# Splits of the transposes moved ahead of the work around them, and eight loads begun from ScalarE's queue, in a two-layer hybrid encoder

## The chip, the cores and the metric

The kernel runs on one core of one Trainium2 chip. The metric is the time of one execution on the device, in microseconds (us), as the median of several runs; lower is better. One further run was taken with the hardware profiler, and all rows shown come from it.

A core has engines that each work through their own instructions strictly in the order in which these were laid down: TensorE (PE in the profile, its weight loads PEld), VectorE (DVE), ScalarE (ACT), GpSimd (POOL) and SyncE (SP). Between engines only semaphores order the work. An engine whose next instruction waits does nothing, even if a later one could run.

## The reference, cut to what matters

A sequence of 512 tokens with 1024 features goes through two layers. Each layer is a token mixer and a channel mixer (FFN), each with a normalisation ahead of it and one behind it:

```python
for layer in range(DEPTH):                       # 2
    hn = rms_norm(x, norm_mix_pre[layer])
    m = retention_na_mixer(hn, ...) if layer % 2 == 0 else ssd_mixer(hn, ...)
    x = x + rms_norm(m, norm_mix_post[layer])
    f = conv_geglu_ffn(rms_norm(x, norm_ffn_pre[layer]), ...)
    x = x + rms_norm(f, norm_ffn_post[layer])
```

The second mixer is the state space layer: its result y (512 x 2048) is multiplied by an output matrix, and what comes out is m. The FFN is an up-projection to 2 x 2816 columns, a convolution over three tokens, gelu(gate) * value, and a down-projection.

## The kernel before, in words

The 512 tokens are four tiles of 128 (t = 0 to 3), which lie on the partitions in `E.x`. A product needs its left operand with features on the partitions, so each normalised tile is transposed on TensorE. All products are made from two-part numbers: `split` (lines 79 to 82) takes a float32 tile and makes a rounded part `hi` with a ScalarE copy (L81) and a rest `lo` with a VectorE subtraction (L82), which needs `hi` first. A product is then three matmuls (`mm3`, L86 to L88): high by high, high by low, low by high. In the rows, `whi` and `wlo` are the parts of a weight, `xh` and `xl` those of the transposed tile, `hh` and `hl` parts that lie in the FFN's own buffers, and `wst` is the buffer in which a weight lands.

From one stage to the next a tile goes through this chain, all of it per tile t and some of it per half of 512 features:

- `post_half` (L144): the sum of squares of a half of m on ScalarE (L119, `junk`, with the result `ssm`), and m times the gain on VectorE (L150, `mg`).
- `post_norm` (L167): 1/rms from both sums (`v_m`, L109, on VectorE, then `r_m`, L111, on GpSimd), and `x = mg * r_m + x` for both halves (L175, VectorE).
- `norm` (L121): sum of squares of x (L119, ScalarE, `ssx`), 1/rms (`v_x`, L109; `r_x`, L111), and `xs = x * r_x * gain` for both halves (L131, VectorE).
- `turn` (L134): for each half four transposes on TensorE into a PSUM tile `pt` (L140), and the split of `pt` into `xh` (L81, ScalarE) and `xl` (L82, VectorE).

`finish` (L152) runs these for the tiles by small tables of steps: x is `post_norm`, s is `norm`, t is `turn`. At the end of the state space layer the table is `TAIL`; the turns of tiles 2 and 3 come from a list `late`, which the next FFN flushes between its first products. Those first products are cut by columns: the FFN first takes tokens 0 to 255 (tiles 0 and 1) of four products: with its first pair of weights (`mm_9234`, `mm_9235` in the built program), then with its second pair (`mm_9236`, `mm_9237`, whose weight parts are `hh` and `hl` and lie where the state space layer's `mg` tiles lay), then tokens 256 to 511 of all four. TensorE's order holds tile 2's transposes between the first and the second pair, and tile 3's among the second pair's products.

In the state space layer's last stage (`out_tile`, L815), `E.x` serves as the accumulator of the output product, and x itself waits in device memory (`xd`). For each tile and half, VectorE adds the last group's product to the accumulator and puts m elsewhere (L828), and then a load brings x back into `E.x` (L829). `post_norm` of the tile needs both loads. All loads of the kernel, these eight and the weights', are begun from SyncE's queue, in order.

The order on each engine is made by a scheduler when the program is built. It follows the order in which the code is written; what is written under `high_priority(n)` ranks n places further ahead. The splits of weights have stood under `high_priority(60)`; the splits in `turn` under none.

Of the kernel before, what the change touches and what calls it, by code (L numbers as in the profile page):

```python
# [25 lines left out]
class Env:  # L26
# [107 lines left out]
    def turn(self, t):  # L134

        nc = self.nc
        for h, xs in enumerate(self.xs[t]):
            pt = self.px.tile([P, 4, P], F32, name="pt", tag="px")
            for j in range(4):
                nc.tensor.transpose(pt[:, j], xs[:, j * P:(j + 1) * P], self.ident)  # L140
            o = (slice(None), slice(h * 4, h * 4 + 4), slice(t * P, (t + 1) * P))
            self.split(self.xh[o], self.xl[o], pt)

    def post_half(self, st, t, n, ps, g_post, eng=None, m=None):  # L144

# [407 lines left out]
def mixer1(E, w_dt, w_fm, cw, dtc, cols, mask, w_out, g_post_row, done):  # L553
# [4 lines left out]
    nc, tc = E.nc, E.tc  # L558
    C = P
    H, H2 = SSD_H, 2 * SSD_H  # L560
    with ExitStack() as ctx:
# [14 lines left out]
        xd = E.dram.tile([NT, P, D], F32, name="xd")  # L576
# [231 lines left out]
        def out_mm(o, t, ws):  # L808
            ps = E.mm.tile([P, 512], F32, name="mm")
            tt = slice(t * P, (t + 1) * P)  # L810
            for k in range(4):
                yh, yl = o["y"][k]
                E.mm3(ps, yh[:, tt], yl[:, tt], *ws[k], k == 0, k == 3)
            return ps

        def out_tile(o, n, t, ws, fin=None, ps=None):
            g = o["g"]
            ns = slice(n * 512, n * 512 + 512)
            if ps is None:
                ps = out_mm(o, t, ws)  # L820
            acc, r = E.x[:, t, ns], o["r"][:, t:t + 1]
            if g == 0:
                nc.scalar.activation(acc, ps, AF.Identity, scale=r)
            elif g < NG - 1:
                nc.vector.scalar_tensor_tensor(acc, ps, r, acc, op0=ALU.mult, op1=ALU.add)
            else:
                m = three.tile([P, 512], F32, name="m", tag="e")
                nc.vector.scalar_tensor_tensor(m, ps, r, acc, op0=ALU.mult, op1=ALU.add)  # L828
                nc.sync.dma_start(acc, xd[t, :, ns])  # L829
                fin(t, n, m)  # L830

        def out(o, n):
            ws = E.wunit(w_out[o["g"], n, 0]) + E.wunit(w_out[o["g"], n, 1])
            for t in range(NT):
                out_tile(o, n, t, ws)
# [48 lines left out]
        def fin(t, n, m):  # L884
            E.post_half(st, t, n, m, g_post, None, four.tile([P, 512], F32, name="mg", tag="z"))
# [7 lines left out]
        for t in range(NT):  # L893
            for n in range(2):
                out_tile(gs[-1], n, t, ws[n], fin, first[n] if t == 0 else None)
            E.finish(TAIL[t], st, done)
# [146 lines left out]
```

## Time and profile before

| what | value |
|---|---|
| median of 3 runs | 1437.23 us |
| lowest and highest of them | 1435.54 and 1437.54 us |
| time of the profiled execution | 1435.78 us |
| its span, from the first to the last instruction | 1434.0 us |
| TensorE busy | 1398.5 us, 98% of the span |
| VectorE busy | 946.3 us, 66% |
| ScalarE busy | 720.3 us, 50% |
| GpSimd busy | 60.6 us, 4% |

How to read the rows: a row of the timeline has the start in us from the beginning of the span, the duration, the engine, the line, the operation, what it writes and reads, and a count where equal instructions were merged. In brackets stands the idle time of the engine just before, and what ended it. In the row of a window stand its length, then for each engine its busy time and number of instructions, then the clock that was granted to TensorE as a share of full speed (PEclk), then the transfers. Matmuls overlap in their pipeline, so their pace is read from the distance of their starts, not from their durations.

### The profile page before, as it was taken

To read this page: it belongs to the slowest core of one execution; us is meant where nothing else is said; L and a number is where in the kernel's file an instruction comes from. 1 tells how busy PE (TensorE), PEld (TensorE's weight loads), DVE (VectorE), ACT (ScalarE), POOL (GpSimd) and SP (SyncE) were. 2 spreads that over 40 slices of the span, in tenths; PEclk is the share of its full clock that TensorE was granted. 3 is DMA by queue.
4 is the path that set the end of the run, shared out by engine and by line. 5 is a ranking of instruction groups with operands and counts; after the bars stand their busy time and mean duration, and the time that the engine had idled before them with its cause. 6 is when DMAs were issued, how large, how long until landed. Compare 5 with 4: busy or idle time off the path is not lost.

```text
span 1434.0 us, 18009 instructions
## 1 busy us (share of the span) xinstructions
PE 1398.5 (98%) x6832; PEld 1141.0 (80%) x6832; DVE 946.3 (66%) x1486; ACT 720.3 (50%) x1192; POOL 60.6 (4%) x67
## 2 busy tenths in 40 slices
PE   7999999999999999999999999999889999999998
PEld 6877777898888888888777787777678888888886
DVE  7368888666566552357889786999886666564242
ACT  5356665454444431334888766577544444443230
POOL 0010110100000000000000000000110000000000
PEclk9999999999999999999999999999999999999999
DMA  7443232233233333332556354345432233333241
GB/s 255 146 141 92 85 96 77 83 108 102 89 98 95 102 94 97 120 107 95 159 180 184 111 176 131 95 153 162 143 120 87 90 100 94 100 89 102 89 132 59
DMA packets 56950, 166.34 MB, mean 116 GB/s; under 512 B 7200, under 2 KB 7968, under 8 KB 56864
## 3 DMA queue, kind: packets, MB, share of 16 engines
q1 hardware_dynamic: 56864, 165.20, 37.2%
q8 instruction: 54, 0.88, 0.2%
q14 instruction: 32, 0.26, 0.1%
HBM read 157.57 MB, written 5.51 MB: 114 GB/s over the span
## 4 chain that ended last, share of the span: by engine, by line
PE 80%; DVE 9%; ACT 5%; DMA 3%; issue 2%; POOL 0%; SPq 0%; DVEq 0%; POOLq 0%; ACTq 0%
PE mm L86 24%; PE mm L87 24%; PE mm L88 24%; DMA pb<-pd 1%; DVE wlo L82 1%; PE st L719 1%; DVE xf L683 1%; PE pt L140 1%; PE y L449 1%; PE pi L762 1%; DMA wst<-in_c_out 1%; PE pt L663 1%; PE py L782 1%; DVE ti L766 1%; DVE yl L795 0%
## 5 line engine op out<-in xcount | busy, mean ns | idle before, releaser
L88 PE MATMUL mm<-xl,whi 128*128 128x512 f32 (+2 forms) x1216 | 463.9, 382 | 4.0 <-DVE xl L82 3.8
L86 PE MATMUL mm<-xh,whi 128*128 128x512 f32 (+2 forms) x1216 | 464.0, 382 | 1.5 <-ACT z L689 0.7
L87 PE MATMUL mm<-xh,wlo 128*128 128x512 f32 (+2 forms) x1216 | 463.4, 381 | 1.4 <-DVE wlo L82 1.4
L82 DVE TENSOR_TENSOR wlo<-wst,whi 128x1024 fp32r<-128x1024 f32 (+1 forms) x208 | 255.5, 1229 | 198.0 <-ACT whi L81 195.8
L81 ACT CAST whi<-wst 128x1024 fp32r<-128x1024 f32 (+1 forms) x208 | 217.3, 1045 | 191.4 <-PE mm L87 119.6
L88 PEld LDWEIGHTS mm<-xl,whi 128*128 128x128 f32 (+1 forms) x1216 | 228.6, 188 | 48.4 <-DVE xl L82 4.5
L86 PEld LDWEIGHTS mm<-xh,whi 128*128 128x128 f32 (+1 forms) x1216 | 229.0, 188 | 46.8 <-issue 2.4
L87 PEld LDWEIGHTS mm<-xh,wlo 128*128 128x128 f32 (+1 forms) x1216 | 229.0, 188 | 45.2 <-DVE wlo L82 2.7
L227 DVE SCALAR_TENSOR_TENSOR cv<-mm,cwt,cv 128x511 f32<-128x511 f32 x88 | 65.7, 747 | 95.2 <-ACT cv L226 94.9
L86 PE MATMUL mm<-whi,hh 128*128 128x512 f32 x288 | 112.0, 389 | 0.0
L87 PE MATMUL mm<-whi,hl 128*128 128x512 f32 x288 | 112.0, 389 | 0.0
L88 PE MATMUL mm<-wlo,hh 128*128 128x512 f32 x288 | 112.0, 389 | 0.0
L226 ACT ACTIVATE cv<-mm,cwt 128x512 f32<-128x512 f32 x88 | 68.4, 777 | 39.8 <-PE mm L88 39.8
L81 ACT CAST hh<-cv 128x512 fp32r<-128x512 f32 x44 | 27.3, 621 | 100.5 <-DVE cv L235 100.3
L233 ACT ACTIVATE cv<-cv 128x512 f32<-128x512 f32 x44 | 27.8, 633 | 85.2 <-DVE cv L228 85.2
L228 DVE SCALAR_TENSOR_TENSOR cv<-mm,cwt,cv 128x511 f32<-128x511 f32 x88 | 66.0, 750 | 3.0
L744 ACT ACTIVATE ds<-um,tok,ddt 128x128 f32<-128x128 f32 x128 | 55.7, 484 | 16.1 <-DVE e L747 15.7
L88 PEld LDWEIGHTS mm<-wlo,hh 128*128 128x128 f32 x288 | 54.1, 188 | 11.3
L87 PEld LDWEIGHTS mm<-whi,hl 128*128 128x128 f32 x288 | 54.1, 188 | 11.2
L86 PEld LDWEIGHTS mm<-whi,hh 128*128 128x128 f32 x288 | 54.1, 188 | 11.2
L82 DVE TENSOR_TENSOR hl<-cv,hh 128x512 fp32r<-128x512 f32 x44 | 30.5, 693 | 28.9 <-ACT hh L81 28.9
L741 ACT ACTIVATE e<-pb,tok 128x128 f32<-128x128 f32 x128 | 43.0, 392 | 11.7 <-DMA pb<-pd 10.2
(236 smaller groups left out, 1945.6 us busy)
## 6 DMA issues: line engine op xcount, KB each, us to landing
wst<-in_f_up SPq DMA_DIRECT2D x88, 512.0 KB
wst<-in_f_down SPq DMA_DIRECT2D x44, 512.0 KB
wst<-in_c_fm SPq DMA_DIRECT2D x40, 512.0 KB
pb<-pd SPq DMA_DIRECT2D x64, 256.0 KB
wst<-in_ab_fm SPq DMA_DIRECT2D x20, 512.0 KB
gain<-yd SPq DMA_DIRECT2D x32, 256.0 KB
wst<-in_c_out SPq DMA_DIRECT2D x16, 512.0 KB
gain<-in_norms SPq DMA_DIRECT2D x8, 512.0 KB
```

The costliest lines, as they stand in the source:

```text
L81: self.nc.scalar.copy(hi, src)
L82: self.nc.vector.tensor_tensor(lo, src, hi.bitcast(F32), op=ALU.subtract)
L86: mm(out, lh, rh, start=first, stop=False)
L87: mm(out, ll, rh, start=False, stop=False)
L88: mm(out, lh, rl, start=False, stop=last)
L140: nc.tensor.transpose(pt[:, j], xs[:, j * P:(j + 1) * P], self.ident)
L226: nc.scalar.activation(o, ps, AF.Identity, scale=w(1), bias=w(3))
L227: nc.vector.scalar_tensor_tensor(o[:, 1:], ps[:, :S - 1], w(0), o[:, 1:], op0=ALU.mult, op1=ALU.add)
L228: nc.vector.scalar_tensor_tensor(o[:, :S - 1], ps[:, 1:], w(2), o[:, :S - 1], op0=ALU.mult, op1=ALU.add)
L233: nc.scalar.activation(g, g, AF.Gelu_apprx_tanh)
L741: nc.scalar.activation(e[:, c], pb[0][:, cc], AF.Identity, scale=-1.0, bias=tok[:, 0, c, h:h + 1])
L744: nc.scalar.activation(ds[:, c], um, AF.Identity, scale=ddt[:, c, h:h + 1], bias=tok[:, 1, c, H + h:H + h + 1])
```

## The change

Two edits. In `turn`, the split of a transposed tile is put under `high_priority(100)`, so that it ranks ahead of the splits of weights (60) and of what stands up to a hundred places before it. In `out_tile`, the eight loads that bring x back are begun from ScalarE's queue and no longer from SyncE's.

```diff
             o = (slice(None), slice(h * 4, h * 4 + 4), slice(t * P, (t + 1) * P))
-            self.split(self.xh[o], self.xl[o], pt)
+            with self.tc.high_priority(100):
+                self.split(self.xh[o], self.xl[o], pt)
...
                 nc.vector.scalar_tensor_tensor(m, ps, r, acc, op0=ALU.mult, op1=ALU.add)
-                nc.sync.dma_start(acc, xd[t, :, ns])
+                nc.scalar.dma_start(acc, xd[t, :, ns])
                 fin(t, n, m)
```

No instruction is added or removed; the numbers of lines behind the first edit rise by one. Orders change in three kinds of places: at the start of the program, in VectorE's part of the two changes of stage inside it (from the first mixer to its FFN, from that FFN to the state space layer, where TensorE's and ScalarE's orders stay as they were), and at the state space layer's end, where all engines but GpSimd are touched. SyncE also begins a few loads in another order at the start and where the state space layer begins.

The first place is VectorE at the start of the program. `wlo_107` and `wlo_114` are the rests of the first two weights, `pt_135` and `pt_142` the two halves of tile 0's transposes, `pt_160` and `pt_167` those of tile 1. Before:

```order
L82 TENSOR_TENSOR wlo_107<-wst_104,whi_106 128x1024
L82 TENSOR_TENSOR xl_99<-pt_135,xh_98 128x4x128
L82 TENSOR_TENSOR xl_99<-pt_142,xh_98 128x4x128
L82 TENSOR_TENSOR wlo_114<-wst_111,whi_113 128x1024
L82 TENSOR_TENSOR xl_99<-pt_160,xh_98 128x4x128
L82 TENSOR_TENSOR xl_99<-pt_167,xh_98 128x4x128
```

And now:

```order
L82 TENSOR_TENSOR xl_99<-pt_135,xh_98 128x4x128
L82 TENSOR_TENSOR xl_99<-pt_142,xh_98 128x4x128
L82 TENSOR_TENSOR wlo_107<-wst_104,whi_106 128x1024
L82 TENSOR_TENSOR xl_99<-pt_160,xh_98 128x4x128
L82 TENSOR_TENSOR xl_99<-pt_167,xh_98 128x4x128
L82 TENSOR_TENSOR wlo_114<-wst_111,whi_113 128x1024
```

Each weight's rest now stands behind the two rests of a tile.

The second place is VectorE at the end of the state space layer, from the split of tile 0's second half (`pt_9107`) to that of tile 1's first half (`pt_9173`). `m_9127` and `m_9148` belong to tile 3, `mg_9057` and `mg_9078` to tile 2, `xs_9037` and `xs_9039` to tile 1; `wlo_9211` is the rest of the FFN's second weight, `v_m_9083` is of tile 2, `v_x_9033` of tile 1 and `v_x_9092` of tile 2. Before:

```order
L82 TENSOR_TENSOR xl_99<-pt_9107,xh_98 128x4x128
L131 SCALAR_TENSOR_TENSOR xs_9037<-x_97,r_x_9035,gain_8969 128x512
L131 SCALAR_TENSOR_TENSOR xs_9039<-x_97,r_x_9035,gain_8969 128x512
L82 TENSOR_TENSOR wlo_9211<-wst_9208,whi_9210 128x1024
L109 TENSOR_SCALAR v_m_9083<-ssm0_9058,ssm1_9079 128x1
L828 SCALAR_TENSOR_TENSOR m_9127<-mm_9114,rg_8945,x_97 128x512
L175 SCALAR_TENSOR_TENSOR x_97<-mg_9057,r_m_9085,x_97 128x512
L175 SCALAR_TENSOR_TENSOR x_97<-mg_9078,r_m_9085,x_97 128x512
L150 TENSOR_TENSOR mg_9130<-m_9127,gain_8881 128x512
L828 SCALAR_TENSOR_TENSOR m_9148<-mm_9135,rg_8945,x_97 128x512
L109 TENSOR_SCALAR v_x_9092<-ssx_9089 128x1
L82 TENSOR_TENSOR xl_99<-pt_9173,xh_98 128x4x128
```

And now:

```order
L82 TENSOR_TENSOR xl_99<-pt_9107,xh_98 128x4x128
L176 SCALAR_TENSOR_TENSOR x_97<-mg_8998,r_m_9026,x_97 128x512
L176 SCALAR_TENSOR_TENSOR x_97<-mg_9019,r_m_9026,x_97 128x512
L82 TENSOR_TENSOR wlo_9211<-wst_9208,whi_9210 128x1024
L829 SCALAR_TENSOR_TENSOR m_9127<-mm_9114,rg_8945,x_97 128x512
L109 TENSOR_SCALAR v_x_9033<-ssx_9030 128x1
L829 SCALAR_TENSOR_TENSOR m_9148<-mm_9135,rg_8945,x_97 128x512
L131 SCALAR_TENSOR_TENSOR xs_9037<-x_97,r_x_9035,gain_8969 128x512
L131 SCALAR_TENSOR_TENSOR xs_9039<-x_97,r_x_9035,gain_8969 128x512
L151 TENSOR_TENSOR mg_9130<-m_9127,gain_8881 128x512
L151 TENSOR_TENSOR mg_9151<-m_9148,gain_8881 128x512
L82 TENSOR_TENSOR xl_99<-pt_9173,xh_98 128x4x128
```

Tile 1's split now comes ahead of tile 2's `v_m`, of its two updates of x and of its `v_x`. Tile 1's own updates of x and `xs`, which stood ahead of the split of `pt_9107` or right behind it, come later by that split and by the weight's rest.

The third place is VectorE right behind the second, up to `hl_9216`, the rest of the FFN's second pair of weights. `xs_9096` and `xs_9098` are tile 2's, `mg_9130` and `mg_9151` tile 3's, and `pt_9286` and `pt_9293` are tile 2's transposes. Before, from tile 2's `xs` on:

```order
L131 SCALAR_TENSOR_TENSOR xs_9096<-x_97,r_x_9094,gain_8969 128x512
L131 SCALAR_TENSOR_TENSOR xs_9098<-x_97,r_x_9094,gain_8969 128x512
L150 TENSOR_TENSOR mg_9151<-m_9148,gain_8881 128x512
L82 TENSOR_TENSOR xl_99<-pt_9180,xh_98 128x4x128
L109 TENSOR_SCALAR v_m_9156<-ssm0_9131,ssm1_9152 128x1
L175 SCALAR_TENSOR_TENSOR x_97<-mg_9130,r_m_9158,x_97 128x512
L175 SCALAR_TENSOR_TENSOR x_97<-mg_9151,r_m_9158,x_97 128x512
L82 TENSOR_TENSOR hl_9216<-wst_9218,hh_9214 128x512
```

And now, from tile 2's `v_m` on:

```order
L109 TENSOR_SCALAR v_m_9083<-ssm0_9058,ssm1_9079 128x1
L176 SCALAR_TENSOR_TENSOR x_97<-mg_9057,r_m_9085,x_97 128x512
L176 SCALAR_TENSOR_TENSOR x_97<-mg_9078,r_m_9085,x_97 128x512
L109 TENSOR_SCALAR v_x_9092<-ssx_9089 128x1
L131 SCALAR_TENSOR_TENSOR xs_9096<-x_97,r_x_9094,gain_8969 128x512
L131 SCALAR_TENSOR_TENSOR xs_9098<-x_97,r_x_9094,gain_8969 128x512
L109 TENSOR_SCALAR v_m_9156<-ssm0_9131,ssm1_9152 128x1
L176 SCALAR_TENSOR_TENSOR x_97<-mg_9130,r_m_9158,x_97 128x512
L82 TENSOR_TENSOR xl_99<-pt_9286,xh_98 128x4x128
L82 TENSOR_TENSOR xl_99<-pt_9293,xh_98 128x4x128
L176 SCALAR_TENSOR_TENSOR x_97<-mg_9151,r_m_9158,x_97 128x512
L82 TENSOR_TENSOR hl_9216<-wst_9218,hh_9214 128x512
```

Tile 2's chain from `v_m` to `xs` now stands behind tile 1's splits, with nothing between its links, and tile 2's two splits stand between the two updates of x of tile 3. On ScalarE, in the same stretch, the casts of tile 2's transposes (`xh`) now stand ahead of the four casts `hh`, where they stood behind them; and the two loads of each tile stand ahead of its sums of squares.

## The prediction

> **What bounds the kernel now.** First the page, for the engine that bounds:
>
> ```profile
> span 1434.0 us, 18009 instructions
> PE 1398.5 (98%) x6832; PEld 1141.0 (80%) x6832; DVE 946.3 (66%) x1486; ACT 720.3 (50%) x1192; POOL 60.6 (4%) x67
> ```
>
> TensorE is idle for 35.5 us in all, so a change of order can win or lose only there. Second the windows, at the places where the order changes:
>
> ```profile
> 10.00:20.00 10.00, 9.39 (x37) 7.63 (x38) 8.64 (x15) 6.75 (x12) 1.25 (x3) 1.00 0.89 319
> 280.00:290.00 10.00, 10.00 (x87) 10.00 (x86) 8.33 (x15) 5.51 (x12) 1.10 (x2) 1.00 0.71 218
> 650.00:660.00 10.00, 9.76 (x82) 9.52 (x81) 4.77 (x9) 3.58 (x8) 0.00 (x0) 1.00 0.01 4
> 1020.00:1030.00 10.00, 5.82 (x44) 4.31 (x42) 7.34 (x11) 7.81 (x12) 1.62 (x1) 0.83 0.53 166
> 1060.00:1070.00 10.00, 6.20 (x38) 5.90 (x39) 8.47 (x16) 3.75 (x9) 1.22 (x3) 0.83 0.52 168
> 1090.00:1400.00 310.00, 310.00 (x1369) 256.65 (x1369) 161.09 (x193) 119.02 (x154) 0.00 (x0) 1.00 0.32 98
> ```
>
> The two changes of stage inside the program (280 to 290, 650 to 660) leave TensorE idle 0.00 and 0.24 us: nothing to win there. The place that counts is 1060 to 1070, with 3.8 us idle and the clock at 0.83. Behind it the second FFN keeps TensorE busy for 310.00 of 310 us, so what it gains or loses at the state space layer's end reaches the end of the program whole. Third, TensorE's waits:
>
> ```profile
> PE pt L140 <- DVE xs L131: 10.5, 5, 7.3
> PE mm L88 <- DVE xl L82: 3.8, 1, 3.8
> ```
>
> The second is the wait that the first edit is about: one wait, 3.8 us, for an `xl`. Fourth, the timeline around it, VectorE and TensorE:
>
> ```profile
> 1043.06 1.41 DVE L828 SCALAR_TENSOR_TENSOR m<-mm,rg,x 128x512 f32<-128x512 f32 x2 [1.14 <-POOL rg L806]
> 1044.38 1.28 DVE L150 TENSOR_TENSOR mg<-m,gain 128x512 f32<-128x512 f32 x2
> 1045.59 0.21 DVE L109 TENSOR_SCALAR v_m<-ssm,ssm 128x1 f32<-128x1 f32 x1
> 1046.49 1.41 DVE L175 SCALAR_TENSOR_TENSOR x<-mg,r_m,x 128x512 f32<-128x512 f32 x2
> 1047.83 0.68 DVE L150 TENSOR_TENSOR mg<-m,gain 128x512 f32<-128x512 f32 x1
> 1049.12 0.15 DVE L109 TENSOR_SCALAR v_x<-ssx 128x1 f32<-128x1 f32 x1
> 1049.95 1.41 DVE L131 SCALAR_TENSOR_TENSOR xs<-x,r_x,gain 128x512 f32<-128x512 f32 x2
> 1050.85 0.63 PE L140 MATMUL pt<-head,xs 128*128 128x128 f32 x4 [0.79 <-DVE xs L131]
> 1058.18 1.22 DVE L82 TENSOR_TENSOR wlo<-wst,whi 128x1024 fp32r<-128x1024 f32 x1
> 1059.32 0.20 DVE L109 TENSOR_SCALAR v_m<-ssm,ssm 128x1 f32<-128x1 f32 x1
> 1062.93 0.68 DVE L82 TENSOR_TENSOR xl<-pt,xh 128x512 fp32r<-128x512 f32 x1
> 1063.67 0.39 PE L88 MATMUL mm<-xl,whi 128*128 128x256 f32 x1 [3.83 <-DVE xl L82]
> 1064.51 0.42 PE L87 MATMUL mm<-xh,wlo 128*128 128x256 f32 x1
> 1064.73 0.41 PE L88 MATMUL mm<-xl,whi 128*128 128x256 f32 x1
> 1067.82 0.28 PE L86 MATMUL mm<-xh,whi 128*128 128x256 f32 x1
> 1067.94 0.28 PE L87 MATMUL mm<-xh,wlo 128*128 128x256 f32 x1
> ```
>
> VectorE runs row on row without a break from 1043.06 until that `xl`: TensorE waits for VectorE's whole queue, not for one badly placed instruction. After the gap matmuls follow each other at 0.22 us, later at 0.12: the clock was halved.
>
> **The start.** The first weight's rest and the first tile's rests change places.
>
> ```profile
> 11.13 1.22 DVE L82 TENSOR_TENSOR wlo<-wst,whi 128x1024 fp32r<-128x1024 f32 x1
> 12.26 1.28 DVE L82 TENSOR_TENSOR xl<-pt,xh 128x512 fp32r<-128x512 f32 x2
> 13.00 0.79 PE L87 MATMUL mm<-whi,xl 128*128 128x512 f32 x1
> 13.60 0.63 PE L88 MATMUL mm<-wlo,xh 128*128 128x512 f32 x1
> 14.02 0.63 PE L86 MATMUL mm<-whi,xh 128*128 128x512 f32 x1
> ```
>
> VectorE comes free at 11.13. `xl` first lets L87 start some 0.4 us earlier; `wlo` is then done at 11.13 + 1.2 + 1.2 = 13.6, when L88 starts now. One more matmul fits ahead of that, at the step of 0.42 us (13.60 to 14.02): −0.4 us. The weights' later rests are hidden by TensorE's full queue. Bounds: 0 to −0.8 (two matmuls).
>
> **Tile 1's split.** VectorE's steps, by distance of starts: m 0.66 (1043.06 to 1044.38, two), mg 0.605 (1044.38 to 1045.59, two), x 0.67 (1046.49 to 1047.83, two), xs the same by its 1.41 for two; xl 0.61 by the row of four `hl` below; `wlo` 1.14 (1058.18 to 1059.32); `v_m` 0.12 and `v_x` 0.08 at most, since next to nothing hides behind them. From the first m to tile 1's first `xl` the new order has 8 m, 8 mg, 4 x, 4 xs, 2 xl, 1 wlo, 2 `v_m`, 2 `v_x`: 5.28 + 4.84 + 2.68 + 2.68 + 1.22 + 1.14 + 0.24 + 0.16 = 18.24 us. Handovers to GpSimd and back take 0.90 (`v_m` 1045.59 to x 1046.49) and 0.83 (`v_x` 1049.12 to xs 1049.95); where one instruction stands between, 0.1 to 0.2 shows, four times: 0.55. So this `xl` starts at 1043.06 + 18.24 + 0.55 = 1061.85, not 1062.93, and TensorE goes on 0.74 later (1062.93 to 1063.67), at 1062.6: only 1.1 us earlier. The edit reorders a full queue; it doesn't empty it.
>
> **What comes late instead.** Tile 2's chain now begins behind tile 1's splits. The FFN's second pair of weights hangs on the end of this chain:
>
> ```profile
> 1067.06 1.41 DVE L175 SCALAR_TENSOR_TENSOR x<-mg,r_m,x 128x512 f32<-128x512 f32 x2 [0.65 <-POOL r_m L111]
> 1068.63 2.18 ACT L81 CAST hh<-wst 128x512 fp32r<-128x512 f32 x4 [4.58 <-issue]
> 1069.28 2.50 DVE L82 TENSOR_TENSOR hl<-wst,hh 128x512 fp32r<-128x512 f32 x4 [0.81 <-ACT hh L81]
> 1070.71 1.06 ACT L119 ACTIVATE junk<-x 128x1024 bf16<-128x1024 f32 x1
> 1071.81 0.28 PE L87 MATMUL mm<-xh,hl 128*128 128x256 f32 x1
> 1072.71 1.41 DVE L131 SCALAR_TENSOR_TENSOR xs<-x,r_x,gain 128x512 f32<-128x512 f32 x2 [0.66 <-POOL r_x L111]
> 1074.56 1.04 PE L140 MATMUL pt<-head,xs 128*128 128x128 f32 x8
> ```
>
> The cast `hh` waited 4.58 us with no releaser named, and began 0.16 us after tile 3's second x ended (1067.06 + 1.41 = 1068.47). Its buffer lies over tile 3's `mg`, so I take that x for its releaser. In the new order: `xl` of tile 1 at 1061.85 and 1062.45; `v_m` of tile 2 at 1063.05; x at +0.90 = 1063.95 and 1064.6; `v_x` 1.96 later (second x 1047.16, `v_x` 1049.12, through ScalarE) = 1066.6; xs at +0.83 = 1067.4 and 1068.1; `v_m` of tile 3 at 1068.75; its first x at 1069.65; then tile 2's two `xl`, 1070.3 and 1070.9; its second x at 1071.5, where it now starts at 1067.73. Then `hh` 0.90 later (1067.73 to 1068.63) = 1072.4, `hl` 0.65 later = 1073.05, and L87 0.75 behind its start = 1073.8. Before, L87 ran at 1071.81, held by TensorE's own work (`hl` began at 1069.28). So the cover of 2 us between `hl` and L87 is used up, and **+2.0 us** is left. Bounds: +1.2, if the small handovers above cost nothing, to +2.8, if they cost twice.
>
> Next, tile 3. Its sum of squares follows the casts by 2.08 (1068.63 to 1070.71), its xs by 2.00 more, its transposes by 0.90: 1072.4 + 4.98 = 1077.4, against 1074.56 with no wait before. That is 2.8 late, **+0.8** on top. What follows (24 products at 0.12, 2.9 us) covers the splits of tile 3.
>
> **The clock.** TensorE's gap moves: no longer 3.83 us before 1063.67, but about 1056.9 to 1060.3 (where nothing is lost, as 1067.4 comes later anyhow), and a second one from about 1069.5 to 1073.8, with one matmul in it. Every gap like it was followed by half clock (the windows of 1020 and 1060, both 0.83: of 10 us, 0.17, or 1.7 us, is lost, which at half speed is a stretch of 3.4 us). At half clock the 23 products between L87 and the transposes take 16 x 0.21 + 7 x 0.12 = 4.2 us and end at 1078.0, not hidden before 1077.4: **+0.6**. Bounds 0 and +1.0. [...]
>
> **The loads from ScalarE's queue.** Eight are taken from SyncE's queue, where only weights that come early enough stood behind them. Now ScalarE has an issue ahead of each sum of squares. ScalarE issues none in this trace; SyncE's rows bound it:
>
> ```profile
> 12.38 0.33 SPq L61 DMA_DIRECT2D wst<-in_ab_v  x1
> 3.66 0.58 SPq L907 DMA_DIRECT2D x<-in_x  x1
> ```
>
> At 0.33 to 0.58 each, tile 1's sums and tile 0's casts come about 1 us later behind tile 2's two loads, just about when VectorE asks for them: +0.1, bounds 0 and +0.5. The wait of each load is for an m that the next sum needs as well. No gain: each x lands long before its use.
>
> **Sum.** −0.4 + 2.0 + 0.8 + 0.6 + 0.1 = +3.1 us. The profiled execution took 1435.78 us (span 1434.0 and 1.78 around it) and becomes 1438.9; the median shown is 1.45 above it, so I predict 1440.3.
>
> **The rivals.**
> [...]
> - *ScalarE becomes the bound.* If an issue there holds it 1 us or more, twice SyncE's rows, both sums of tile 1 and both casts of tile 0 come 1 us later, and with them all of VectorE's queue: +3.9, 1441.1. Decides from about 0.7 us each. Nothing in the trace speaks for it but that ScalarE has not done it.
> - *Faster: the gap closes and nothing takes its place.* If `hh` hangs on something else that is early, and ScalarE and VectorE reach `hh` and `hl` by 1069.3 as now, TensorE keeps the 1.1 us, spares the half clock (3.4 us at half, 1.7) and gains 0.4 at the start: −3.2, 1434.0. For it: the profile names no releaser. Against: even then `hl` stands behind tile 2's splits on VectorE, at 1072 or so; it needs `hl` 2 us sooner.
> - *The scheduler's moves are all hidden*: 1437.2. Against: 3.8 us later for tile 3's x is more than the cover of 2.
>
> **How the numbers follow.** A measurement can tell about 0.2% of 1437.23, 2.9 us, so "slower" begins at 1440.1, close to the forecast. Forecast 0.50 (its own range, from its bounds, 1439.2 to 1441.4; 0.32 of it beyond 1440.1); no half clock 0.22 (0.04 beyond); ScalarE 0.15, all beyond; faster 0.07; hidden 0.06. So slower 0.32 + 0.04 + 0.15 = 0.51, same 0.42, faster 0.07. The range leaves out the faster case and the outer ends: 1437.0 to 1442.4.
>
> **What would show it.** Right: the 3.8 us wait for `xl` is gone, TensorE waits instead for `xs` of tile 1 (about 3 us) and for `hh` and `hl` (about 4 us together); tile 3's second x starts some 3.8 us later, counted from the first m; the start gains 0.4. Wrong: `hh` begins before that x ends, or TensorE reaches the second pair's L87 less than 29 us after the first m (1071.81 − 1043.06 = 28.75 now; 30.7 forecast), or ScalarE's rows between 1050 and 1055 are spread by its loads.

## The result, and the profile after

The changed kernel takes 1437.95 us as the median of 20 runs, the kernel before 1434.51 us as the median of 20 runs beside them. The ratio is 1.0022, with a 95% interval of 1.0015 to 1.0028: slower by 3.2 us (0.0022 x 1434.5). The forecast was +3.1 us, slower. The kernel before ran some 2.7 us faster in these 20 runs than in the three that the forecast started from (1437.23), so the absolute number, 1440.3, is too high by about that; 1437.95 lies within the range. The ratios below leave out one execution of the kernel before, which took 2277.32 us at a granted clock of 0.576.

The profiled execution took 1437.89 us. First the page, after:

```profile
span 1436.1 us, 17999 instructions
PE 1399.1 (97%) x6832; PEld 1141.9 (80%) x6832; DVE 946.5 (66%) x1486; ACT 719.9 (50%) x1192; POOL 60.9 (4%) x67
```

The span is 2.1 us longer, TensorE's busy time 0.6 us. The work is the same, so 1.5 us went into idle time, and the rest into slower matmuls. Now the windows after; the second number of a row is TensorE's busy time, the third from the end the granted clock:

```profile
1060.00:1070.00 10.00, 8.10 (x58) 7.77 (x56) 6.74 (x14) 4.66 (x11) 1.62 (x3) 0.87 0.25 90
1070.00:1080.00 10.00, 8.11 (x53) 7.92 (x54) 6.40 (x11) 5.25 (x9) 0.54 (x1) 0.83 0.32 105
1090.00:1400.00 310.00, 310.00 (x1378) 257.01 (x1377) 161.90 (x193) 119.68 (x155) 0.00 (x0) 1.00 0.32 99
```

And the one row of before that was not shown:

```profile
1070.00:1080.00 10.00, 10.00 (x88) 10.00 (x87) 6.97 (x11) 4.84 (x9) 0.54 (x1) 1.00 0.50 159
```

From 1060 to 1070 TensorE gained 1.9 us of busy time; from 1070 to 1080, where it had been full at full clock, it lost 1.9 us and ran at 0.83. The second FFN behind is full as before, so nothing is made up there. TensorE's waits after name what it waits for:

```profile
PE pt L140 <- DVE xs L131: 13.2, 5, 7.4
...
PE mm L86 <- ACT hh L81: 3.4, 1, 3.4
...
PE mm L87 <- DVE hl L82: 0.3, 1, 0.3
```

The wait of 3.8 us for an `xl` is gone from the list. In its place stand 3.4 us for the cast `hh` and 0.3 for its rest, none of which was there before, and 2.7 us more for `xs` (10.5 before). The timeline after, VectorE, ScalarE and TensorE, shows why `hh` is late (lines of the code are one higher behind the first edit):

```profile
1041.20 1.41 DVE L829 SCALAR_TENSOR_TENSOR m<-mm,rg,x 128x512 f32<-128x512 f32 x2 [1.14 <-POOL rg L807]
1060.21 1.46 DVE L82 TENSOR_TENSOR xl<-pt,xh 128x512 fp32r<-128x512 f32 x2
1061.60 0.21 DVE L109 TENSOR_SCALAR v_m<-ssm,ssm 128x1 f32<-128x1 f32 x1
1065.91 1.42 DVE L131 SCALAR_TENSOR_TENSOR xs<-x,r_x,gain 128x512 f32<-128x512 f32 x2 [0.66 <-POOL r_x L111]
1068.10 0.75 DVE L176 SCALAR_TENSOR_TENSOR x<-mg,r_m,x 128x512 f32<-128x512 f32 x1 [0.65 <-POOL r_m L111]
1068.77 1.28 DVE L82 TENSOR_TENSOR xl<-pt,xh 128x512 fp32r<-128x512 f32 x2
1069.97 0.74 DVE L176 SCALAR_TENSOR_TENSOR x<-mg,r_m,x 128x512 f32<-128x512 f32 x1
1070.87 2.18 ACT L81 CAST hh<-wst 128x512 fp32r<-128x512 f32 x4 [2.11 <-DVE x L176]
1071.53 2.50 DVE L82 TENSOR_TENSOR hl<-wst,hh 128x512 fp32r<-128x512 f32 x4 [0.82 <-ACT hh L81]
1071.54 0.38 PE L86 MATMUL mm<-xh,hh 128*128 128x256 f32 x1 [3.45 <-ACT hh L81]
1072.27 0.39 PE L87 MATMUL mm<-xh,hl 128*128 128x256 f32 x1 [0.35 <-DVE hl L82]
1074.95 1.41 DVE L131 SCALAR_TENSOR_TENSOR xs<-x,r_x,gain 128x512 f32<-128x512 f32 x2 [0.66 <-POOL r_x L111]
1076.86 0.60 PE L140 MATMUL pt<-head,xs 128*128 128x128 f32 x4
1084.41 0.78 ACT L227 ACTIVATE cv<-mm,cwt 128x512 f32<-128x512 f32 x1
```

The last row is the first step behind the four cut products, the FFN's convolution; before it stood here:

```profile
1082.33 0.78 ACT L226 ACTIVATE cv<-mm,cwt 128x512 f32<-128x512 f32 x1
```

The reader is to see the chain that the forecast drew: tile 1's two `xl`, then tile 2 from `v_m` to `xs` with nothing between but handovers, tile 3's first x, tile 2's two rests, tile 3's second x, and 0.90 us behind its start the cast. This time the profile names the releaser of `hh`, that x. Counted from the first m (1043.06 before, 1041.20 now), in us:

| step | before | forecast | after |
|---|---|---|---|
| tile 1's first xl | 19.87 | 18.79 | 19.01 |
| tile 3's second x | 24.67 | 28.4 | 28.77 |
| hh | 25.57 | 29.3 | 29.67 |
| L87 of the second pair | 28.75 | 30.7 | 31.07 |
| tile 3's transposes | 31.50 | 34.9 | 35.66 |
| first convolution | 39.27 | – | 43.21 |

The state space layer's end thus costs 3.9 us. The first m itself comes 1.9 us earlier than before, so that 2.1 us are left at the end. About 1 of those 1.9 us was there already behind the program's start (below). The rest came inside the state space layer, ahead of where its order changes, and differs from execution to execution: the first m stands between 1040.0 and 1043.8 in the twelve profiled executions.

### The profile page after: what moved, and what is told of

The parts are those of the page before. It is cut to its first block, busy times and chain, and to the rows that moved or that the text cites. A ratio compares the mean times of both kernels' runs of the same rounds, so it can differ in the third digit from the quotient of the medians.

```text
span 1436.1 us, 17999 instructions
## 1 busy us (share of the span) xinstructions
PE 1399.1 (97%) x6832; PEld 1141.9 (80%) x6832; DVE 946.5 (66%) x1486; ACT 719.9 (50%) x1192; POOL 60.9 (4%) x67
## 4 chain that ended last, share of the span: by engine, by line
PE 83%; DVE 7%; ACT 4%; DMA 3%; issue 2%; POOL 1%; SPq 0%; DVEq 0%; POOLq 0%; ACTq 0%
PE mm L87 25%; PE mm L86 25%; PE mm L88 25%; PE st L720 1%; DVE wlo L82 1%; PE pi L763 1%; PE pt L140 1%; PE y L450 1%; PE py L783 1%; DMA wst<-in_c_out 1%; DVE xf L684 1%; DMA pb<-pd 1%; PE pt L664 1%; DMA wst<-in_c_fm 1%; DVE x L176 1%
## 5 line engine op out<-in xcount | busy, mean ns | idle before, releaser
L87 PE MATMUL mm<-xh,wlo 128*128 128x512 f32 (+2 forms) x1216 | 463.5, 381 | 1.7 <-DVE wlo L82 1.7
L87 PEld LDWEIGHTS mm<-xh,wlo 128*128 128x128 f32 (+1 forms) x1216 | 228.9, 188 | 45.9 <-DVE wlo L82 3.0
L87 PE MATMUL mm<-whi,hl 128*128 128x512 f32 x288 | 112.0, 389 | 0.0
L87 PEld LDWEIGHTS mm<-whi,hl 128*128 128x128 f32 x288 | 54.1, 188 | 11.1
```

Of the source, the lines that this page charges most:

```text
L87: mm(out, ll, rh, start=False, stop=False)
```

## The experiments

Theory A is the forecast's: the splits' rank delays tile 3's second x, `hh` hangs on it, and TensorE waits for `hh`. The rivals stand in the expectations. All ratios are to the kernel before, run beside each kernel; "first m to" means the distance in that kernel's profiled execution, from its timeline.

| kernel | ratio, 95% interval | first m to tile 3's second x | to the cast behind it | to the first convolution |
|---|---|---|---|---|
| before | 1 | 24.67 | 25.57 | 39.27 |
| changed | 1.0022 (1.0015 to 1.0028) | 28.77 | 29.67 | 43.21 |
| e1, first edit alone | 1.0019 (1.0010 to 1.0028) | 28.43 | 29.32 | 43.66 |
| e2, second edit alone | 1.0004 (0.9995 to 1.0012) | 25.95 | 26.86 | 40.09 |
| e3, start alone | 0.9997 (0.9989 to 1.0006) | 25.01 | 25.90 | 40.34 |
| e4, changed, third weight elsewhere | 0.9998 (0.9988 to 1.0008) | 26.70 | 27.66 | 38.94 |
| e5, before, third weight elsewhere | 1.0005 (0.9994 to 1.0017) | 26.44 | 27.34 | 41.74 |
| e6, e1 without tile 2's part | 0.9999 (0.9987 to 1.0010) | 26.85 | 27.75 | 41.58 |
| e7, tile 1 alone, third weight elsewhere | 0.9987 (0.9976 to 0.9999) | 27.04 | 27.93 | 37.98 |
| e8, turns earlier, third weight elsewhere | 0.9976 (0.9965 to 0.9988) | 26.45 | 27.35 | 37.41 |
| e9, changed without tile 2's part | 1.0003 (0.9994 to 1.0012) | 27.36 | 28.27 | 41.02 |
| e10, turns earlier alone | 0.9993 (0.9985 to 1.0002) | 25.58 | 26.75 | 39.42 |

The last column needs care, for it depends on how much half clock each execution happened to have. Between the first m and the convolution TensorE had half clock for 3.4 us in the executions of before, e2, e4 and e7 to e10, for 6.8 us in those of the changed kernel, e1, e3 and e6, and for 10.2 us in that of e5. Where TensorE has no idle time, 3.4 us at half clock do the work of 1.9: products of 256 columns follow each other there at 0.21 us, and at 0.12 otherwise (changed kernel, 1073.26 to 1073.47 and 1076.38 to 1076.50).

**e1 and e2: which edit.** e1 undoes the second edit, e2 the first:

```diff
-                nc.scalar.dma_start(acc, xd[t, :, ns])
+                nc.sync.dma_start(acc, xd[t, :, ns])
```

> The first edit alone: the splits of the transposes under high_priority(100), the eight loads back on SyncE's queue. Theory A (the splits' rank delays tile 3's second x, the casts hh hang on that x, and TensorE waits): nearly the whole loss stays, +2.4 to +3.6 us against the kernel before (ratio 1.0017 to 1.0025), and TensorE's wait for hh of about 3 us is in the profile. Rival B (the eight issues on ScalarE hold up the sums of squares and with them VectorE's queue): the loss goes with them, and what is left is the gain at the start, -0.4 to -1.0 us (ratio 0.9993 to 0.9997).

> The second edit alone: the eight loads from ScalarE's queue, the splits ranked as in the kernel before. Theory A: within 0.5 us of the kernel before (ratio 0.9996 to 1.0004), tile 3's second x and the casts hh where they were, within 0.5 us counted from the first m. Rival B: +3 to +4 us (1.0021 to 1.0028), the sums of squares behind the issues start late.

With the first edit alone nearly the whole loss stays, 1.0019, and so does TensorE's wait, here in e1's list:

```profile
PE mm L86 <- ACT hh L81: 3.4, 1, 3.4
```

With the second alone the time is not told apart from before. Rival B is out. But e2's profile is not what theory A expected in one point. Its timeline:

```profile
1040.87 1.41 DVE L828 SCALAR_TENSOR_TENSOR m<-mm,rg,x 128x512 f32<-128x512 f32 x2 [1.14 <-POOL rg L806]
1066.14 1.41 DVE L175 SCALAR_TENSOR_TENSOR x<-mg,r_m,x 128x512 f32<-128x512 f32 x2 [0.65 <-POOL r_m L111]
1067.72 2.18 ACT L81 CAST hh<-wst 128x512 fp32r<-128x512 f32 x4 [3.39 <-DVE x L175]
1070.43 0.28 PE L87 MATMUL mm<-xh,hl 128*128 128x256 f32 x1
```

`hh` begins 26.86 us behind the first m, 1.3 later than before, not within 0.5: the loads do move the chain. TensorE doesn't wait for it, since the cover of 2 us between `hl` and L87 is not used up: TensorE itself reaches this L87 0.8 us later than before, so most of the cover is left. An issue of these loads on ScalarE takes what it took on SyncE (0.32 in the trace of before), 0.35 and 0.33 in e2's first two rows:

```profile
1041.65 0.35 ACTq L829 DMA_DIRECT2D x<-xd  x1
...
1042.31 0.33 ACTq L829 DMA_DIRECT2D x<-xd  x1
```

**e3: the start.** The rank holds only while the input's four tiles are turned (`place` is 0 until the first mixer begins), and the loads are on SyncE's queue:

```diff
-            self.split(self.xh[o], self.xl[o], pt)
+            with self.tc.high_priority(100) if self.place == 0 else ExitStack():
+                self.split(self.xh[o], self.xl[o], pt)
```

> The higher rank at the start of the program alone (the four tiles of the input), everything later as in the kernel before, loads on SyncE's queue. Theory A: a gain of 0.4 us by the prediction's term, of up to 1.0 us by the distance that the profiled executions show behind the start (ratio 0.9993 to 0.9997). A rival by which the start is where the time is lost: slower, 1.001 or more.

The ratio, 0.9997, fits a gain of 0.4 us but can't be told from nothing. The traces can tell more. The first step of the first mixer's core, of before and after, on TensorE:

```profile
L433 PE MATMUL sc<-rq,rk x32: 389/389/496, 88.0 to 228.5; 128*128 128x512 f32 x32
```

```profile
L434 PE MATMUL sc<-rq,rk x32: 389/393/497, 86.9 to 227.5; 128*128 128x512 f32 x32
```

It starts at 86.7 to 87.2 in the nine kernels with the rank at the start (86.9 in the changed one, 87.2 in e3), and at 87.7 to 88.0 in the three without it (before, e2, e5). So the start gains 0.5 to 1.3 us, about 0.9. The windows from 12 to 16 us show where, before and after:

```profile
12.00:16.00 4.00, 4.00 (x11) 2.91 (x10) 3.94 (x7) 2.06 (x5) 0.00 (x0) 1.00 0.89 308
```

```profile
12.00:16.00 4.00, 4.00 (x14) 3.04 (x14) 3.99 (x6) 3.24 (x7) 0.00 (x0) 1.00 0.87 306
```

Fourteen matmuls begin there instead of eleven, where the forecast counted one more. But not all of this is order. The step from matmul to matmul falls from 0.43 to 0.23 us at 16.16 before, and already at 14.67 after; TensorE was at half pace until then, though the windows give 1.00. Before and after:

```profile
16.16 0.45 PE L87 MATMUL mm<-whi,xl 128*128 128x512 f32 x1
16.45 0.40 PE L88 MATMUL mm<-wlo,xh 128*128 128x512 f32 x1
```

```profile
14.67 0.43 PE L87 MATMUL mm<-whi,xl 128*128 128x512 f32 x1
14.93 0.40 PE L88 MATMUL mm<-wlo,xh 128*128 128x512 f32 x1
```

In e3 and e5 the step falls at the same time, 15.7. There the rank gives one matmul more by then, as forecast, and 0.6 us at the mixer's core (87.2 against 87.8). So about 0.6 of the 0.9 is order; the rest goes with full pace coming sooner. It came at 14.5 to 15.7 with the rank and at 15.7 to 16.2 without; whether the rank brings that about is not shown.

**e4 and e5: what `hh` hangs on.** One number decides which weights' parts lie in the FFN's own buffers (in both layers' FFNs). The third weight of the four, the first of the second pair, goes to a buffer of `whi` and `wlo` instead, e4 in the changed kernel and e5 in the kernel before:

```diff
-        w0 = [[E.wunit(w_up[s, f], extra() if 2 * f + s >= 2 else None) for s in range(2)] for f in range(2)]
+        w0 = [[E.wunit(w_up[s, f], extra() if 2 * f + s >= 3 else None) for s in range(2)] for f in range(2)]
```

> The changed kernel, with one number changed: the parts of the FFN's third weight (the first of the second pair) no longer lie in the FFN's own buffers, over the state space layer's, but in a buffer of whi and wlo, which is free by then; the fourth weight stays where it was. No work is added or removed. Theory A (that cast waits for nothing but the buffers' release by tile 3's second x): the cast begins before that x, TensorE's wait of 3.4 us for hh is gone, and 3 to 4.5 us come back: 0 to -1.2 us against the kernel before (ratio 0.9992 to 1.0000). Rival D (the rest of that weight is late anyhow, since VectorE's queue holds it behind tile 2's splits): at most 1 us comes back, +2.4 us or more against the kernel before (1.0017 or more).

> The kernel before, with the third weight's parts in a buffer of whi and wlo as in e4. Theory A: there the first products of the second pair wait for nothing (2 us lay between hl and L87), so the same number changes next to nothing: -0.8 to +0.4 us against the kernel before (ratio 0.9994 to 1.0003). Rival E (the other buffer helps for a reason of its own, whatever the order of the splits): about as much as it gave e4 against the changed kernel, -3 us (0.998).

e4 takes back the whole loss (0.9998), e5 changes nothing that can be told (1.0005; by its median +0.7 us, a little above the expected +0.4). e5's late convolution, 41.74, is no wait for a cast, of which TensorE's waits in its trace show none, but goes with its 10.2 us at half clock. e4's timeline on ScalarE, the two casts of weights in one row and the fourth weight's `hh`, and all waits of TensorE from 1056 to 1082:

```profile
1055.46 2.01 ACT L81 CAST whi<-wst 128x1024 fp32r<-128x1024 f32 x2
...
1071.44 1.14 ACT L81 CAST hh<-wst 128x512 fp32r<-128x512 f32 x2
```

```profile
PE pt L140 <- DVE xs L131: 4.3, 2, 3.7
```

The third weight's cast runs at 1055.5, 15 us ahead of tile 3's second x (1070.48 here); the fourth's still follows that x. TensorE waits for no cast. Rival D, and E with e5, are out. One reserve: with that cast early, the order on VectorE changed as well, and tile 2's rests stand behind tile 3's second x in e4. So e4 alone doesn't part the buffer from those rests, and in its profiled execution one stretch of half clock fewer helps it as well.

**e6 and e9: tile 2's rests.** The rank is taken from tile 2 alone, at the state space layer's end (`place` is 2 from there on), e6 with the loads on SyncE's queue, e9 with them on ScalarE's:

```diff
-            with self.tc.high_priority(100):
+            with self.tc.high_priority(100) if self.place < 2 or t != 2 else ExitStack():
                 self.split(self.xh[o], self.xl[o], pt)
```

> The first edit without its part for tile 2 at the state space layer's end: tile 2's two splits rank there as in the kernel before, all others under high_priority(100); loads on SyncE's queue, the third weight where it was. Theory A: without tile 2's two rests (1.2 us) ahead of tile 3's second x, this x and the casts hh come 1.2 us earlier than in e1, and with less half clock 1.2 to 1.8 us of the 2.7 come back: +0.9 to +1.5 us against the kernel before (ratio 1.0006 to 1.0011). A rival by which tile 1's splits alone push tile 3's chain beyond the cover: as e1, +2.4 us or more (1.0017).

> The changed kernel with both edits, but tile 2's two splits at the state space layer's end rank as in the kernel before: the part that e6 left out of the first edit, left out of the whole change. The question is what tile 2's rests ahead of tile 3's second x cost. By the prediction's sum they are 1.2 us of its 3.8, and with the half clock behind them 1.2 to 1.8 us of the loss: +1.6 to +2.3 us against the kernel before (ratio 1.0011 to 1.0016). By e6's median they are the whole loss: within 0.6 us of the kernel before (0.9996 to 1.0004).

Tile 3's second x comes 1.6 us earlier than in e1, and 1.4 earlier than in the changed kernel, about as expected from two rests of 0.6. But more of the time comes back than was expected: e6 0.9999, e9 1.0003. From the changed kernel to e9 that is 0.0019 x 1434.5 = 2.7 us by the ratios, 2.2 us by the first convolution. e9's timeline, its waits and its window show the surplus (lines there are one higher again, so L87 is the product high by high):

```profile
1066.88 1.42 DVE L177 SCALAR_TENSOR_TENSOR x<-mg,r_m,x 128x512 f32<-128x512 f32 x2 [0.65 <-POOL r_m L112]
1068.21 1.28 DVE L83 TENSOR_TENSOR xl<-pt,xh 128x512 fp32r<-128x512 f32 x2
1068.46 2.18 ACT L82 CAST hh<-wst 128x512 fp32r<-128x512 f32 x4 [0.33 <-DVE x L177]
1070.17 0.39 PE L87 MATMUL mm<-xh,hh 128*128 128x256 f32 x1 [0.66 <-ACT hh L82]
```

```profile
PE mm L87 <- ACT hh L82: 2.3, 2, 1.7
```

```profile
1070.00:1080.00 10.00, 9.61 (x79) 9.44 (x80) 5.89 (x10) 3.72 (x7) 0.54 (x1) 1.00 0.49 159
```

TensorE's waits for `hh` are 1.7 and 0.66 us, and the clock stays at 1.00, where the changed kernel had 0.83. So in these two executions tile 2's rank costs twice: 1.4 us of chain, and a gap that is followed by half clock. What the other tiles' rank takes from tile 3's chain is not quite inside the cover: counted from the first m, the second pair's first product with `hl` comes 1.5 us later than before in e9 and 0.9 in e6, against a gain of about 0.9 at the start. In e6's own profiled execution the clock was halved there all the same (0.83 from 1070 to 1080; 41.58 to the convolution), and by the intervals anything from 1.1 to 4.3 us may come back from e9; its expectation of 1.2 to 1.8 us back is at the low end of that. The rival of e6, that tile 1's splits alone make the loss (1.0017 or more), is out.

**e7, e8 and e10: a better order.** e7 gives the rank at the state space layer's end to tile 1 alone (`t == 1` in place of `t != 2`; ahead of that all tiles have it), with the loads on SyncE's queue and the third weight moved. e8 gives the rank at the start alone, as e3, moves the third weight, and begins the turns of tiles 0 and 1 a step earlier; e10 is e8 without the third weight's move:

```diff
-TAIL = ("x0 s0", "x1 s1", "x2 s2 t0", "x3 s3 t1")
+TAIL = ("x0 s0", "x1 s1 t0", "x2 s2 t1", "x3 s3")
```

> A version built on theory A: the higher rank at the start and between the stages inside the program, and at the state space layer's end for tile 1 alone; loads on SyncE's queue; the third weight in a buffer of whi and wlo. Tile 1's first xl is early, tile 2's chain pays for one pair of splits only, and no cast waits for tile 3's x where TensorE needs it: -2 to -3.5 us against the kernel before (ratio 0.9976 to 0.9986). If VectorE's queue is full whatever stands first in it: -0.4 to -1 us (0.9993 to 0.9997), from the start alone.

> The higher rank at the start alone, loads on SyncE's queue, the third weight in a buffer of whi and wlo, and in the table of the state space layer's end the turns of tiles 0 and 1 one step earlier (x1 s1 t0, then x2 s2 t1), so that the splits come earlier with the transposes they belong to and not by rank. Theory A: as e7 or a little better, -2 to -3.5 us against the kernel before (0.9976 to 0.9986). If only a split's rank can close TensorE's gap before the first xl: -0.4 to -1 us (0.9993 to 0.9997).

> e8 without the third weight's other buffer: the higher rank at the start alone, and the turns of tiles 0 and 1 one step earlier in the table of the state space layer's end. Theory A: the first xl is early, but the casts hh hang on tile 3's second x as in the kernel before, so TensorE waits there for what it won, and only the start's gain is left: -1 to +0.5 us (ratio 0.9993 to 1.0003). A rival by which the order of the turns alone makes e8's gain and the buffer adds nothing: -2.5 to -3.5 us (0.9976 to 0.9983).

e8 is the fastest of all, 0.9976: 3.4 us faster than before. e7 gains 1.9 us, a little less than the 2 to 3.5 expected. e10, at 0.9993, gains 1.0 us and can't be told from before: with the same table of turns, the third weight's buffer is worth 0.0017, or 2.4 us (0.4 to 4.5 by the intervals; 2.0 by the first convolution). TensorE's waits from 1056 to 1080, e8 first and then e10:

```profile
PE pt L141 <- DVE xs L132: 2.6, 2, 2.2
```

```profile
PE mm L87 <- ACT hh L82: 1.9, 2, 1.2
PE pt L141 <- DVE xs L132: 1.7, 1, 1.7
PE mm L89 <- DVE xl L83: 0.4, 1, 0.4
```

This is the pair that parts the buffer from the order, which e4 did not: tile 3's second x is even 0.9 us earlier in e10 than in e8 (25.58 against 26.45), and only e10 waits for `hh`. The two orders on VectorE are not equal everywhere, but in both of them tile 2's rests stand behind that x.

## Why the prediction was right, step by step

- *The edit reorders a full queue; it doesn't empty it.* Shown. Tile 1's first `xl` is 0.86 us earlier (1.1 forecast), against a wait of 3.8.
- *`hh` hangs on tile 3's second x.* Shown: in ten of the eleven other kernels the cast into the FFN's buffers begins 0.89 to 0.96 us behind that x, as before, wherever the x stands (25.01 to 28.77 us behind the first m). In e10 it is 1.17, behind two casts `xh`. Where the weight that TensorE needs first doesn't hang there, no wait for it is left (e4, e7, e8).
- *The cover of 2 us is used up, and L87 is 2.0 us late.* Measured 2.3. e2 moves the same chain by 1.3 us, and TensorE doesn't wait for it. e6 moves it by 2.2, and there TensorE does wait, 2.9 us in two pieces, as it comes to `hh` sooner; its ratio shows no loss.
- *Tile 3 and the clock, +0.8 and +0.6.* The first is right, the second too small. Tile 3's `xs` start at 1074.95, 33.75 us behind the first m. Transposes that wait for `xs` start 0.90 behind it (1049.95 to 1050.85 before), so these could start at 1075.85. That is 3.15 later than before, and 0.8 more than L87's 2.3. They start at 1076.86, behind products at half clock: the clock cost 1.0 us, at the upper bound of its term. e9, without the second half clock, shows the same term from the other side.
- *The loads, +0.1.* Not told apart from nothing in time (e2: +0.6, from -0.7 to +1.7; the changed kernel against e1: +0.0003). The reason given was too simple: they shift the chain by 1.3 us in e2, which is hidden there by the cover.
- *The start, -0.4.* Too small: 0.9 by the traces, beyond its bound of -0.8. The one matmul and about 0.6 us are the order's; the rest goes with full pace coming sooner, which the sum did not have. In time e3 can't tell it from nothing.
- *The rivals.* The half clock did return (0.50 from 1072.86 to 1076.27); the 0.22 for its staying away was the author's estimate. ScalarE was not the bound: an issue took 0.34 us, half of the 0.7 from which it would have decided. The gap did not close for good: `hl` began at 1071.53, while TensorE had stood idle from 1068.10 on. And the moves were not all hidden.

So the sum came out right with two terms that were off in opposite directions, 0.5 us too little gain at the start and 0.4 too little loss at the clock. The mechanism is shown; that +3.1 met 3.2 so closely is partly luck.

## What to carry to other kernels

A wait on an engine that runs row on row is not closed by putting the awaited instruction first: everything that it passes becomes late by its length, so look for the next consumer of what was passed, here a cast that waits for buffers to come free, and count its cover. Give the rank only to the split that is awaited: tile 1's was, tile 2's was not, and leaving that one out took back most of the loss. And a buffer taken over from the stage before is a hidden wait for that stage's last reader. Look for both kinds of wait: here the better order alone (e10, with the start's gain in it) and the other buffer alone (e5) can't be told from before, and both together (e8) gained 3.4 us.

## What the runs showed of the hardware

In the executions shown here half clock came behind gaps of TensorE, but not behind every gap. Windows of the changed kernel, cut at the ends of the slow stretches:

```profile
1059.20:1062.61 3.41, 3.38 (x16) 3.34 (x17) 2.67 (x6) 1.79 (x4) 0.54 (x1) 0.50 0.79 291
...
1069.44:1072.86 3.42, 0.97 (x6) 0.78 (x7) 2.60 (x6) 1.99 (x4) 0.00 (x0) 1.00 0.00 0
1072.86:1076.27 3.41, 3.41 (x19) 3.41 (x18) 2.63 (x5) 1.25 (x3) 0.54 (x1) 0.50 0.67 199
```

In the 3.42 us ahead of the second slow stretch six matmuls ran, 0.97 us of it, and the next 3.41 us had half clock, though TensorE was busy throughout. The two slow stretches begin 13.66 us apart. A gap of 3.45 us ended at 1071.54, 1.3 us ahead of the fall. In e10 a shorter one came ahead of a slow stretch: its longest gap there was 1.74 us, and by this profile TensorE was busy for 1.77 of the 3.41 us before:

```profile
1055.66:1059.07 3.41, 1.77 (x12) 1.35 (x12) 2.98 (x7) 1.22 (x4) 0.66 (x1) 1.00 0.67 222
1059.07:1062.49 3.42, 2.98 (x14) 2.70 (x14) 3.29 (x6) 1.27 (x4) 0.54 (x1) 0.50 0.29 86
```

In e2 a longer gap, of 2.51 us, ended at 1057.58, and the products behind it came at the full step (0.12 us from 1059.16 to 1059.28 and from there to 1059.40). Only behind the next gap, of 2.90 us, which ended at 1062.58, did the step rise to 0.21 us (1063.94 to 1064.15). e6 and e9 differ too: in e6 TensorE waited for `hh` for 2.24 and 0.66 us, and the clock from 1070 to 1080 was 0.83; in e9 it waited for 1.67 and 0.66 us, and the clock was 1.00. So the length of the longest gap alone does not tell whether the clock falls, and what does is not shown.

The clock also makes single profiles differ. e3 has the same orders at the state space layer's end as the kernel before, but half clock for 6.8 us there instead of 3.4 (a granted clock of 0.66 from 1060 to 1070, against 0.83), and its first convolution came 1.07 us later:

```profile
1060.00:1070.00 10.00, 8.68 (x53) 8.64 (x53) 8.05 (x15) 5.12 (x13) 1.30 (x3) 0.66 0.41 130
```

Half clock does not always cost. In the layer's last group, whose order e1 leaves as it was, e1 had half clock for 10.2 us and the kernel before for 3.4 (from 1015 to 1040 a granted clock of 0.80 and 0.93). Yet from the last accumulated product (1011.76 and 1014.67) to the first m it took 28.3 us in e1 and 28.4 before.

The medians of the kernel before ran from 1434.51 to 1435.71 us in the four sets of runs, so ratios of kernels run beside each other were needed, and distances inside a stage, to say anything about terms of 0.5 us.
